# Row sums of a 64 MB tensor: which rows each partition owns

## The chip, the cores and the metric

The kernel runs on one core of one Trainium2 chip. The metric is the device time of one execution in microseconds (us). Before the change the median of three runs is 161.98 us (161.95 to 162.12).

## What is computed

The reference sums each row of 1024 numbers and multiplies the sum by 0.5.

```python
batch, seq, dim = 32, 512, 1024
x = np.random.randn(batch, seq, dim).astype(np.float32)
return (np.sum(x, axis=-1) * multiplier).astype(np.float32)   # multiplier 0.5
```

There are 16384 rows of 4 KB each: 67.1 MB are read, 64 KB are written.

## The kernel before

The 16384 rows are shared out to 128 partitions, 128 rows each. A partition owns 112 consecutive rows of the first 14336 (`x_rows`, `out_rows`: partition p starts at row 112p) and 16 consecutive rows of the last 2048 (`x_last`, `out_last`: partition p starts at row 14336 + 16p). All 128 sums of a partition are gathered in one tile `res`, from which two stores go out.

The loop at line 95 runs over seven blocks of 16 columns. Each round allocates a tile `xb` (128 partitions x 16 rows x 1024 numbers, 8.4 MB) from a pool of three buffers and loads it with one DMA from SyncE's queue (line 98). A partition's part of such a load is 16 rows that lie one after the other in DRAM, 64 KB. VectorE sums the tile with one reduction (line 100) and scales the sums into `res` (line 103). In the seventh block VectorE takes rows 0 to 7 only, and ScalarE takes the other eight, a row at a time, with an activation that accumulates (line 74).

The eighth block is the last 2048 rows. It comes in five DMAs of falling size: rows 0 to 7, 8 to 12 and 13 to 14 (line 117), and row 15 in two parts (line 123) into a tile of its own, `end`. Its rows are summed one at a time, on VectorE (line 84) and on ScalarE (line 74). The first 112 columns of `res` are stored while this block is still coming (line 127, the "early" store); the other 16 are stored at the end (line 145).

The order of the work is that of the code, engine by engine. The first three loads find free buffers and wait for nothing; a hook (`start_loads_at_entry`) puts them at the very start of SyncE's program, ahead of its start barrier. Load 4 and later ones wait on SyncE until VectorE (for the last pieces: VectorE, then ScalarE for the early store) has released a buffer. All loads and stores go through the one queue of SyncE.

## Time and profile before

| | us |
|---|---|
| median of the runs | 161.98 |
| span of the profiled execution | 160.2 |
| VectorE busy | 119.3 (74%) |
| ScalarE busy | 17.3 (11%) |
| one reduction of a full tile (line 100) | 17.22 |
| first full tile landed | 21.89 |
| last DMA of the input landed | 157.55 |

The span runs from SyncE's first DMA issue to the last instruction of the profiled execution. The runs' time holds 1.78 us more than it (161.98 - 160.20), which lies around the span. "To landing" is the time from a DMA's issue to the completion of all of its 16 parts; a load that stands behind others in the queue has their time in it too.

### The profile page before, as it was taken

What the parts mean: (1) busy time and instruction counts of PE and PEld (TensorE: products, weight loads), DVE (VectorE), ACT (ScalarE), POOL (GpSimd) and SP (SyncE); (2) the same over time, 40 slices, a digit from 0 to 9 for tenths busy, and PEclk for the clock granted to TensorE, in tenths of its full rate; (3) what the DMA queues carried; (4) which work ended last, traced back from release to release, by engine and by line L of the source; (5) the groups of instructions that cost most, each with busy time, mean ns of one, the idle gap of its engine ahead of it and who ended that gap; (6) DMA issues with size and microseconds to landing.
All of it is one profiled execution on the core that took longest, in us unless ns stands there. A gap on an engine that the chain in (4) does not pass through costs nothing.

```text
span 160.2 us, 139 instructions
## 1 busy us (share of the span) xinstructions
DVE 119.3 (74%) x35; ACT 17.3 (11%) x31; POOL 0.2 (0%) x4
## 2 busy tenths in 40 slices
DVE  0000059998799968999599995999959999597543
ACT  0000000000000000000000000000000000599952
POOL 0000000000000000000000000000000000000000
DMA  8996996996996997997998989979969969999992
GB/s 278 507 524 262 524 524 262 524 524 262 524 507 278 524 475 311 524 442 344 524 425 360 524 360 425 524 327 458 524 295 491 524 278 507 393 401 422 424 395 76
DMA packets 2016, 67.18 MB, mean 419 GB/s; under 512 B 480, under 2 KB 608, under 8 KB 736
## 3 DMA queue, kind: packets, MB, share of 16 engines
q1 hardware_dynamic: 2016, 67.18, 97.6%
HBM read 67.11 MB, written 0.07 MB: 419 GB/s over the span
## 4 chain that ended last, share of the span: by engine, by line
DMA 75%; DVE 22%; SPq 1%; issue 0%; DVEq 0%
DMA xb<-in_x_dram 51%; DMA end<-in_x_dram 24%; DVE sums L100 22%; SPq L117 1%; SPq L123 0%; DVE end L84 0%; SPq L98 0%; DVE res L103 0%; DVEq L208 0%
## 5 line engine op out<-in xcount | busy, mean ns | idle before, releaser
L100 DVE TENSOR_REDUCE sums<-xb 128x16 f32<-128x16384 f32 (+1 forms) x7 | 112.0, 16002 | 31.5 <-DMA xb<-in_x_dram 31.5
L74 ACT ACT_TABLE_LOAD x1 | 1.3, 1283 | 138.0 <-DMA xb<-in_x_dram 138.0
L74 ACT ACTIVATE xb<-xb 128x1024 f32<-128x1024 f32 x15 | 15.7, 1044 | 2.1 <-DMA xb<-in_x_dram 2.1
L84 DVE CUSTOM_DVE_ANT_0 xb<-xb 128x512 f32<-128x512 f32 x8 | 5.1, 690 | 4.9 <-DMA xb<-in_x_dram 4.9
L74 ACT ACTIVATION_READ_ACCUMULATOR xb<-xb 128x1 f32 x15 | 2.8, 187 | 0.0
L55 DVE MEMSET end<- 128x2 f32 x1 | 0.1, 60 | 1.8 <-PEq L194 1.8
L103 DVE TENSOR_SCALAR res<-sums 128x16 f32<-128x16 f32 (+1 forms) x7 | 1.2, 174 | 0.2
L84 DVE CUSTOM_DVE_ANT_0 end<-end 128x272 f32<-128x272 f32 (+1 forms) x2 | 0.9, 426 | 0.2 <-DMA end<-in_x_dram 0.2
L84 DVE DVE_READ_ACCUMULATOR2_ANT res<- 128x1 f32 x9 | 0.7, 83 | 0.0
L194 POOL MEMSET const-bfloat16-1.0<- 128x1 bf16 x1 | 0.1, 102 | 0.0
L194 POOL MEMSET const-uint8-127<- 128x1 uint8 x1 | 0.1, 102 | 0.0
L194 POOL MEMSET const-float32-0.0<- 128x1 f32 x1 | 0.1, 99 | 0.2 <-issue 0.2
L194 POOL MEMSET const-float32-1.0<- 128x1 f32 x1 | 0.1, 99 | 0.0
L84 DVE DVE_READ_ACCUMULATOR2_ANT end<- 128x1 f32 x1 | 0.1, 83 | 0.0
## 6 DMA issues: line engine op xcount, KB each, us to landing
xb<-in_x_dram SPq DMA_DIRECT2D x1, 4096.0 KB, 31.1
xb<-in_x_dram SPq DMA_DIRECT2D x1, 2560.0 KB, 36.9
xb<-in_x_dram SPq DMA_DIRECT2D x1, 1024.0 KB, 38.9
end<-in_x_dram SPq DMA_DIRECT2D x1, 272.0 KB, 39.0
end<-in_x_dram SPq DMA_DIRECT2D x1, 240.0 KB, 39.2
xb<-in_x_dram SPq DMA_DIRECT2D x7, 40.8
out_dram<-res SPq DMA_DIRECT2D x1, 56.0 KB, 10.0
out_dram<-res SPq DMA_DIRECT2D x1, 8.0 KB, 1.4
```

The source lines that it names most:

```text
L55: nc.vector.memset(end[:, at - 2 : at], 0.0)
L74: acts.append(nc.scalar.activation(out=t[:, r, :], in_=t[:, r, :], func=mybir.ActivationFunctionType.Copy, scale=mul, accum_out=res[:, col ...
L84: return nc.vector.tensor_tensor_reduce(out=row[:, 0:mid], in0=row[:, 0:mid], in1=row[:, mid:], scale=scale, scalar=0.0, op0=ADD, op1=ADD, ...
L100: nc.vector.reduce_sum(out=sums[:, c0 : c0 + h], in_=t[:, 0:h, :], axis=mybir.AxisListType.X)
L103: nc.vector.tensor_single_scalar(out=res[:, c0 : c0 + h], in_=sums[:, c0 : c0 + h], scalar=mul, op=mybir.AluOpType.mult,)
L117: nc.sync.dma_start(out=t[:, lo:hi, :], in_=x_last[:, lo:hi, :])
L194: nc = _bacc.Bacc("TRN2", target_bir_lowering=False, num_devices=1)
```

## The change

```diff
     own = rows - B
-    x_rows = x_flat[0 : P * own, :].rearrange("(p c) d -> p c d", p=P)
+    x_rows = x_flat[0 : P * own, :].rearrange("(b g c) d -> g b c d", b=4, c=own)
     x_last = x_flat[P * own : N, :].rearrange("(p c) d -> p c d", p=P)
-    out_rows = out_flat[0 : P * own].rearrange("(p c) -> p c", p=P)
+    out_rows = out_flat[0 : P * own].rearrange("(b g c) -> g b c", b=4, c=own)
...
-        loads.append(nc.sync.dma_start(out=t, in_=x_rows[:, c0 : c0 + B, :]))
+        loads.append(nc.sync.dma_start(out=t, in_=x_rows[:, :, c0 : c0 + B, :]))
```

The first 14336 rows are still cut into 128 runs of 112 rows. Run number r went to partition r; now run 32b + g goes to partition 4g + b (b from 0 to 3, g from 0 to 31). So four neighbouring partitions own runs that are 32 runs (14.7 MB) apart, and partitions 4 apart own neighbouring runs (458,752 bytes apart). The early store writes the sums back by the same rule. The tiles in SBUF, the sums, the scaling and the last 2048 rows are as they were.

## Prediction

> **What bounds the kernel now.** I read the page first: the busy shares, the slices and the DMA queue.

> ```profile
> span 160.2 us, 139 instructions
> ## 1 busy us (share of the span) xinstructions
> DVE 119.3 (74%) x35; ACT 17.3 (11%) x31; POOL 0.2 (0%) x4
> ...
> DMA  8996996996996997997998989979969969999992
> ...
> q1 hardware_dynamic: 2016, 67.18, 97.6%
> ```

> The busiest engine is at 74%, while the one DMA queue holds its 16 engines for 97.6% of the span. The 9s and 6s of the DMA row are long packets booked in the slice where they start, not gaps. Next the chain that ended last, in order of time:

> ```profile
> 0.00 0.38 SPq L98
> 0.38 0.05 issue
> 0.43 40.77 DMA xb<-in_x_dram
> ...
> 118.38 39.17 DMA end<-in_x_dram
> 157.55 0.02 issue
> 157.58 0.41 DVE end L84
> ```

> It starts with SyncE's first issue, ends with the last transfer landing at 157.55, and is a DMA at both ends. The two reductions in its middle are there only because a load waits for a buffer before it queues up behind others. That this wait costs nothing is read from the timeline, where each reduction starts when its tile has landed, and from VectorE's waits:

> ```profile
> 21.91 17.22 DVE L100 TENSOR_REDUCE sums<-xb 128x16 f32<-128x16384 f32 x1 [20.04 <-DMA xb<-in_x_dram]
> ...
> 41.23 17.22 DVE L100 TENSOR_REDUCE sums<-xb 128x16 f32<-128x16384 f32 x1 [1.89 <-DMA xb<-in_x_dram]
> ...
> 60.58 17.22 DVE L100 TENSOR_REDUCE sums<-xb 128x16 f32<-128x16384 f32 x1 [1.92 <-DMA xb<-in_x_dram]
> ```

> Tiles come every 19.35 us (21.91 to 41.23 to 60.58), VectorE needs 17.22 + 0.17 and idles the other 1.9. A buffer is free at 39.3, and by then the queue still holds the rest of load 2 and all of load 3, some 21 us of work. The kernel is one stream of input with a start and an end.

> The trace's packet records show the stream from inside. Each load is 128 packets of 64 KB, 8 per DMA engine. Load 1 takes 2.52 us a packet in the mean, loads 2 to 7 take 2.42 each, from 2.418 to 2.460. That evenness says that each engine runs at its own pace (65,536 B in 2.418 us, 27.1 GB/s, 434 GB/s for 16) and none waits for memory. The only uneven packets are the first of each engine: 16 packets that start between 1.01 and 1.51 us, take 2.77 to 3.47 (mean 3.21), and end between 3.97 and 4.62. Every later packet follows at its engine's pace, so the start's delay is carried to the end.

> By the profile: 21.89 until load 1 has landed + 6 x 19.345 to load 7 (137.96) + 19.59 for the last block (157.55) + 0.02 + 0.41 for the last sum + 2.2 for the last store and the end = 160.2; the 1.78 around the span make 161.98.

> **The change, part by part.**

> *Bytes, packets, sums.* Nothing is added or removed: seven loads, 64 KB contiguous per partition, the same 7 reductions, 7 scalings, activations and stores. Cost 0.

> *The addresses read at one time.* An engine's packets keep their partitions; what moves is where in DRAM the 16 engines stand at one time. If an engine serves groups of four neighbouring partitions, engines stood 4 x 448 KB = 1.75 MB apart and now stand 448 KB apart. In 48 packets in a row (loads 2 to 7) the old spacing costs nothing that can be seen: 2.418 is the floor in all six loads. The last block, unchanged, has a spacing of 4 x 64 KB, and its 32 KB packets take 1.213 us, also 27.0 GB/s. So two spacings, one wider and one narrower than the new one, run at full pace, and I take 0 for the stream. The lower bound is 0 too (the floor can't fall below what each engine shows alone: 2.414 between starts); the upper bound is far, and is rival A.

> [...]

> *The start.* The first 16 packets take 0.79 us more than later ones in the mean. Some of it belongs to any first read: the six 8 KB instruction fetches that the records show ahead of the span take 0.44 to 0.56 us, where 8 KB in the stream takes 0.31 to 0.32, so 0.12 to 0.25 more. The rest, about 0.6, may be 16 engines meeting at memory. If the new spacing took all that away, the last engine would end its first packet at 1.51 + 2.42 + 0.25 = 4.18 instead of 4.62: a gain of 0.44. If it were twice as bad, a loss of 0.6. I take 0: the same spacing of addresses stands at all later packets and costs nothing there, so the start's excess comes more likely from starting than from the spacing.

> Only the first load pays this: its packets start at 1.01, 0.63 after its issue ends, with no work in the queue before. It moves the whole stream by 0.22. Loads 2 and 3 are issued behind it with 19 us of transfers queued. The entry of SyncE grows from 1.33 by 0.66, which delays the start barrier; VectorE's memset at 1.81 waits on that, but VectorE's first tile lands at 21.89. Loads 4 to 7 are issued into a queue with some 21 us of work. Without that cover, each would cost 0.22.

> *The early store.* 128 packets of 448 B at 25 ns, 8 per engine, 0.2 us of each engine, as before. On SyncE it is issued at 147.79; behind it stand only the wait for the last loads (157.55) and the last store, 9.4 us of cover. Cost 0.

> *Sum.* 160.20 + 0.22 = 160.42 in the profile; 161.98 + 0.22 = 162.20 us in the runs. No stall changes place: VectorE still waits 1.9 per tile.

> **Rivals.**

> *A: the stream gets slower.* If the new addresses make engines meet at memory, or if the two-dimensional source is dealt to the engines differently, so that two write through one way into SBUF, packets take longer than 2.418. Each engine has 56 such packets, all on the path, so 1 ns per packet costs 0.056 us; 6 ns (0.25%) is enough for 0.2% of the time. At 1% more (24 ns) the time is 162.20 + 1.35 = 163.6; if all packets were like the first ones (+0.79), +44 us; if pairs shared one way, 56 x 2.418 = +135 us. It also has VectorE as a limit that stays away: its tile of 17.4 is hidden in all of these. Against it: both neighbouring spacings run at the floor.

> [...]

> *B: the start gets faster.* The first packets meet less. The time is 161.98 + 0.22 - 0.44 = 161.76, or 161.54 if the issue costs nothing as well. It decides when the last first-packet ends before 4.4 us. For it: the excess beyond a lone read, 0.6, is there. Against it: the even stream.

> *C: the change does nothing measurable.* Issue 0, start 0: 161.98. It is the lower end of my forecast case.

> **How the numbers follow.** A measurement of this kernel can tell about 0.2% (0.32 us) from no change. Forecast with C, the stream as it is and an issue that costs 0 to 0.38 or a little more: 0.50; its point of 0.22 lies inside 0.2%, its upper third outside: 0.32 same, 0.18 slower. Rival A: 0.24, of which 0.23 slower, 0.01 same, most of it small. Rival B: 0.26, 0.21 faster (it includes a stream floor that falls a little, which I have no row for), 0.05 same. Together faster 0.21, same 0.38, slower 0.41. The range goes from 161.5 (B at its best) to 163.0 (issue 0.38 and a start 0.6 worse: 162.96; or A with 14 ns per packet). Half of A and a little of B lie outside. The likeliest case alone has 161.98 to 162.36.

> **What would show it.** SyncE's first issue should grow from 0.38 to about 0.6 and the isolated ones from 0.33 likewise; the first reduction should start about 0.2 later than 21.91; the reductions should still be 19.35 apart, and VectorE's idle time before each 1.9. Wrong if packets of loads 2 to 7 leave 2.418 (A), if the first packets end well before 4.6 (B), or if the issue keeps its 0.38 (C).

## The result, and the profile after

The changed kernel takes 162.79 us (median of four runs, 162.64 to 162.84) against 162.00 for the one before: 0.79 us more, a ratio of 1.0049 with a 95% interval of 1.0034 to 1.0063. The prediction was 162.2 with a range of 161.5 to 163.0: the range holds the time and the direction is right, but the change costs over three times the 0.22 that the sum gave, and it is slower by more than 0.2%, for which the text had a chance of 0.41 while its point lay within 0.2%.

The page of after, the lines that answer to those of before:

```profile
span 161.1 us, 139 instructions
## 1 busy us (share of the span) xinstructions
DVE 119.3 (74%) x35; ACT 17.3 (11%) x31; POOL 0.2 (0%) x4
...
q1 hardware_dynamic: 2016, 67.18, 97.1%
```

The engines do what they did (VectorE 119.3 and ScalarE 17.3 in both); the span is 0.9 longer and the queue's share is 97.1% instead of 97.6%. So the time is not in the work. The chain that ended last, in order of time (start, length, what), and VectorE's reductions in the timeline:

```profile
0.00 0.66 SPq L98
0.66 0.05 issue
0.70 41.37 DMA xb<-in_x_dram
...
119.24 39.16 DMA end<-in_x_dram
158.40 0.04 issue
158.44 0.41 DVE end L84
```

```profile
22.75 17.22 DVE L100 TENSOR_REDUCE sums<-xb 128x16 f32<-128x16384 f32 x1 [20.02 <-DMA xb<-in_x_dram]
...
42.10 17.22 DVE L100 TENSOR_REDUCE sums<-xb 128x16 f32<-128x16384 f32 x1 [1.92 <-DMA xb<-in_x_dram]
...
61.45 17.22 DVE L100 TENSOR_REDUCE sums<-xb 128x16 f32<-128x16384 f32 x1 [1.92 <-DMA xb<-in_x_dram]
```

The first reduction starts at 22.75 instead of 21.91, 0.84 late. The next are 19.35 apart with 1.92 of idle time before them, as in before, and the last transfer lands at 158.40 instead of 157.55, 0.85 late. Nothing was lost between: all of it is there when load 1 lands.

The issues of line 98 in the answer for tile xb (min/median/max in ns), before and then after:

```profile
L98 SPq DMA_DIRECT2D xb<-in_x_dram x7: 327/328/432, 0.0 to 97.2; - x7
```

```profile
L98 SPq DMA_DIRECT2D xb<-in_x_dram x7: 534/536/656, 0.0 to 98.0; - x7
```

Isolated issues went from 0.33 to 0.54, the first (the first line of each chain) from 0.38 to 0.66. That is 0.27 for the one that counts, and leaves some 0.6 of the 0.84. The packet records of load 1 have the rest:

| first packet of each of the 16 engines, us | before | after |
|---|---|---|
| starts | 1.01 to 1.51 | 1.44 to 1.72 |
| takes (mean) | 2.77 to 3.47 (3.21) | 2.89 to 3.88 (3.21) |
| ends | 3.97 to 4.62 | 4.36 to 5.49 |
| all 64 KB packets behind them, mean | 2.420 | 2.420 |

The packets start 0.4 us later in the mean (1.56 instead of 1.15). Their mean duration did not change, but the ends are spread over 1.13 us instead of 0.65. Load 1's last packet ends at 21.53 before and at 22.39 after, 0.86 later, and VectorE starts on it 0.84 later, so the end of the slowest first packet (0.87 later) is what counts. From its end to the last landing there are 152.93 us before (157.55 - 4.62) and 152.91 after (158.40 - 5.49).

### The profile page after: what moved, and what is told of

It reads as the page before. It is cut to its first block, busy times and chain, and to the rows that moved or that the text cites. A ratio compares the mean times of both kernels' runs of the same rounds, so it can differ in the third digit from the quotient of the medians.

```text
span 161.1 us, 139 instructions
## 1 busy us (share of the span) xinstructions
DVE 119.3 (74%) x35; ACT 17.3 (11%) x31; POOL 0.2 (0%) x4
## 2 busy tenths in 40 slices
DMA packets 2016, 67.18 MB, mean 417 GB/s; under 512 B 480, under 2 KB 608, under 8 KB 736
## 3 DMA queue, kind: packets, MB, share of 16 engines
q1 hardware_dynamic: 2016, 67.18, 97.1%
## 4 chain that ended last, share of the span: by engine, by line
DMA 75%; DVE 22%; SPq 1%; issue 0%; DVEq 0%
DMA xb<-in_x_dram 51%; DMA end<-in_x_dram 24%; DVE sums L100 21%; SPq L117 1%; SPq L98 0%; SPq L123 0%; DVE end L84 0%; DVE res L103 0%; DVEq L208 0%
## 5 line engine op out<-in xcount | busy, mean ns | idle before, releaser
L100 DVE TENSOR_REDUCE sums<-xb 128x16 f32<-128x16384 f32 (+1 forms) x7 | 112.0, 16001 | 31.5 <-DMA xb<-in_x_dram 31.5
L84 DVE CUSTOM_DVE_ANT_0 xb<-xb 128x512 f32<-128x512 f32 x8 | 5.1, 689 | 5.0 <-DMA xb<-in_x_dram 5.0
L84 DVE CUSTOM_DVE_ANT_0 end<-end 128x272 f32<-128x272 f32 (+1 forms) x2 | 0.9, 426 | 0.2 <-DMA end<-in_x_dram 0.2
L84 DVE DVE_READ_ACCUMULATOR2_ANT res<- 128x1 f32 x9 | 0.7, 83 | 0.0
L84 DVE DVE_READ_ACCUMULATOR2_ANT end<- 128x1 f32 x1 | 0.1, 83 | 0.0
```

The lines of the kernel that those rows point to most:

```text
L84: return nc.vector.tensor_tensor_reduce(out=row[:, 0:mid], in0=row[:, 0:mid], in1=row[:, mid:], scale=scale, scalar=0.0, op0=ADD, op1=ADD, ...
L100: nc.vector.reduce_sum(out=sums[:, c0 : c0 + h], in_=t[:, 0:h, :], axis=mybir.AxisListType.X)
```

## The experiments

Theory I: the longer issue of load 1 is the whole loss. Theory II: the issue makes one half, and the addresses at which the 16 engines start make the other. Rival III (the prediction's rival A): every load pays a little. All times are medians; before, run beside them on the same chip, is 161.98 to 162.02. The distances between engines, here and in the expectations, rest on the prediction's supposition that an engine serves four neighbouring partitions. No trace shows which partitions an engine serves; what the runs vary is the number of rows from partition to partition.

**Where in the stream: load 1 or the others.** Load 1 keeps the old pattern, all others have the new one (`e1_first_old`); then the reverse (`e2_first_new`, with the two sources exchanged, and the two stores' targets with them):

```diff
-        loads.append(nc.sync.dma_start(out=t, in_=x_rows[:, c0 : c0 + B, :]))
+        src = x_rows[:, c0 : c0 + B, :] if b == 0 else x_new[:, :, c0 : c0 + B, :]
+        loads.append(nc.sync.dma_start(out=t, in_=src))
...
-    early = nc.sync.dma_start(out=out_rows, in_=res[:, 0:own])
+    early0 = nc.sync.dma_start(out=out_rows[:, 0:B], in_=res[:, 0:B])
+    early = nc.sync.dma_start(out=out_new[:, :, B:own], in_=res[:, B:own])
```

> Load 1 keeps the old pattern (128 counted steps, the mark, the old addresses), loads 2 to 7 have the new one; the early store is cut in two, so that each part goes to the rows its columns came from. Theory I (all of the loss is the start of load 1, and comes from its issue): 162.0 us, the first issue 0.38 us, the first reduction at 21.9, the issues of loads 2 to 7 0.54 or more and costing nothing. Theory II (the loss is at the start, half from the issue, half from the addresses that the 16 first packets read): 162.0 too. Rival III (the new addresses or the longer issues cost in every load): 162.6 to 162.8, the reductions still later with each load.

> The mirror image: only load 1 has the new pattern, loads 2 to 7 the old one; the early store is cut in two. Theories I and II: the whole loss, 162.8 us, first reduction at 22.7. Rival III: 162.0 to 162.2.

Measured: 162.08 (ratio 1.0008, 0.9999 to 1.0016) and 162.96 (1.0059, 1.0046 to 1.0073). The answer for tile xb shows six long issues (median 536) and a short first one (378) in e1_first_old, and the reverse in e2_first_new:

```profile
L101 SPq DMA_DIRECT2D xb<-in_x_dram x7: 378/536/689, 0.0 to 97.3; - x7
```

```profile
L101 SPq DMA_DIRECT2D xb<-in_x_dram x7: 327/328/666, 0.0 to 98.4; - x7
```

Six loads with the new addresses and the longer issues cost nothing that can be told from noise (162.08), and one, the first, costs all of it (162.96). Rival III falls.

**Issue or addresses.** `e3_first_unmarked` is the kernel before with load 1 built without the mark; `e4_first_near` is the kernel before with load 1 at 28 rows from partition to partition, in a plain pattern with the mark, so that partitions 0, 4, 8 and so on read from where they read in after (that an engine's first packet belongs to one of these is supposed, not shown):

```diff
+        nc.dge_precook = b > 0          # e3
         loads.append(nc.sync.dma_start(out=t, in_=x_rows[:, c0 : c0 + B, :]))
```

```diff
+    x_near = x_flat[0 : P * 28, :].rearrange("(p c) d -> p c d", p=P)      # e4
...
-        loads.append(nc.sync.dma_start(out=t, in_=x_rows[:, c0 : c0 + B, :]))
+        src = x_near[:, 0:B, :] if b == 0 else x_rows[:, c0 : c0 + B, :]
+        loads.append(nc.sync.dma_start(out=t, in_=src))
```

> The kernel before with one thing changed: load 1 is issued without the mark of a shape prepared at build time; addresses and pattern are the old ones. Theory I: nearly the whole loss, 162.6 to 162.8 us, first issue about 0.6 us, first packets ending as late as after the change (5.5 us). Theory II: 162.3 to 162.4, the first packets start 0.2 to 0.4 later but take no longer than before (last end 4.9 to 5.0). Rival III: 162.0 to 162.3.

> The kernel before with one thing changed: load 1 reads partition p from row 28p instead of 112p, with the plain pattern and the mark kept. [...] The first 16 columns are sums of other rows. Theory I: 162.0 us, first packets as before (last end 4.6 us). Theory II: 162.3 to 162.4, first issue 0.38, but first packets take up to 3.9 us and the last ends at about 5.0. Rival III: 162.0.

Measured: e3 162.28 (1.0017, 1.0008 to 1.0026), e4 162.49 (1.0034, 1.0022 to 1.0047). Added, 0.28 + 0.49 = 0.77 of the 0.79. Theory II had expected 162.3 to 162.4 for both: the issue costs a little less than that and the addresses a little more. The beginning of the chain of e3, then of e4:

```profile
0.00 0.54 SPq L99
0.54 0.06 issue
0.59 40.92 DMA xb<-in_x_dram
41.52 0.02 issue
41.54 17.23 DVE sums L101
```

```profile
0.00 0.37 SPq L100
0.37 0.06 issue
0.43 41.18 DMA xb<-in_x_dram
41.61 0.02 issue
41.63 17.23 DVE sums L102
```

In e3 the issue takes 0.54 and load 2's reduction starts at 41.54 instead of 41.23; in e4 the issue is as short as ever (0.37) and the reduction starts later still, at 41.63. In the packet records e3's first packets start late (1.32 to 2.25) and end at 4.33 to 4.88, no more spread than before (0.55); e4's have the old earliest start (1.00) and end at 4.07 to 5.02 (0.95). About a third of the loss (0.28 of 0.77) comes from load 1 without the mark, whose packets start later, and two thirds (0.49) from its addresses, with which the last first packet ends later. Theory I falls; theory II holds, though not with equal halves. Two things stay loose: load 1's issue in after is 0.12 longer than in e3, which the second counted dimension may account for (not tried alone), and e2's time is 0.17 above that of after (first reduction at 23.1, where 22.7 was expected), with overlapping intervals.

**Which addresses.** Only load 1's distance between partitions changes, in the plain pattern of e4: in `P * 28` the 28 becomes 16, 113, 29, 20 or 56; or the whole pattern is moved (`x_flat[4096 : 4096 + P * 28, :]`).

> As the run with 28 rows (plain pattern, mark kept, only load 1 touched, first 16 columns sums of other rows), with 16 rows from partition to partition: load 1 reads one unbroken 8.4 MB, engines 256 KB apart (2^18 bytes). Theory N (the nearer the engines read, the worse the first packets): 162.5 to 162.8 us, last first packet ends at 5.0 us or later. Theory L (it is the lowest address bits in which the engines differ: above bit 18 as before good, bits 16 and 17 bad): 162.0, last end 4.6. Theory P (no order, each set of addresses has its own luck): anything from 161.8 to 162.6.

> The same with 113 rows instead of 112 from partition to partition: engines are as far apart as before (1.77 MB), but their addresses differ from bit 14 up instead of bit 18. Theory N: 162.0 us, last end 4.6. Theory L: 162.5 or more, last end 5.0 or later. Should differing low bits help instead (engines spread over more of memory at once): 161.6 to 161.8, last end 4.2 to 4.4.

> The same with 29 rows: engines as near as after the change (464 KB), addresses that differ from bit 14 up. Theory N: 162.5 us as with 28 rows. Theory L: 162.5 or more. Should differing low bits help: below 162.3, last end under 4.8.

> Only load 1 touched, plain pattern, mark kept, first 16 columns sums of other rows: 20 rows from partition to partition (engines 320 KB apart). 16 rows cost nothing, 28 and 29 cost 0.49 us, 112 and 113 nothing. If the bad distances are a band around 450 KB: 162.0 to 162.2 us. If every distance but multiples of 256 KB and long ones is bad: 162.5.

> The same with 56 rows (engines 896 KB apart, twice the distance after the change). A narrow band around 450 KB: 162.0 us. A loss that fades between 450 KB and 1.75 MB: 162.2 to 162.4.

> 28 rows from partition to partition as in the run of that distance, but the whole pattern starts 4096 rows (16.8 MB) further on. If the distances between the engines make the loss: 162.5 us, last first packet ends at 5.0. If the absolute addresses do: another time, 162.0 as likely as 162.5.

| rows from partition to partition in load 1 | time, us | ratio, 95% interval | last first packet ends, us |
|---|---|---|---|
| 16 | 162.11 | 1.0006, 0.9997 to 1.0015 | 4.58 |
| 20 | 162.19 | 1.0014, 1.0005 to 1.0023 | 5.07 |
| 28 | 162.49 | 1.0034, 1.0022 to 1.0047 | 5.02 |
| 28, moved by 4096 rows | 162.61 | 1.0036, 1.0023 to 1.0048 | 5.36 |
| 29 | 162.50 | 1.0035, 1.0023 to 1.0048 | 5.04 |
| 56 | 162.56 | 1.0036, 1.0022 to 1.0050 | 5.09 |
| 112 (before) | 162.00 | | 4.62 |
| 113 | 162.06 | 1.0003, 0.9994 to 1.0012 | 4.63 |

Nearness (theory N) falls with 16 rows, the lowest differing address bit (L) with 113. A narrow band around 450 KB falls with 56 rows, which cost as much as 28. What is left is a broad band that begins between 16 and 28 rows and ends between 56 and 112, or no order at all (P); the runs do not decide between them. The cost is about the same for 28 and 29 rows and for both places of 28, so neither the exact distance matters there nor this move of the whole pattern. The move is 2^24 bytes, which leaves the low 24 bits of every address as they were; other moves were not tried. Why 28 to 56 rows are bad and 16 and 112 are not is open. No distance tried was better than the one before. The last column is one profiled execution each; that of 20 rows took 162.42, above its median of 162.19.

**Does the start have to be from rest?** Load 1 is cut in two, one 4 KB row per partition from the old addresses first, then 15 rows from the near ones (`e11_row_then_near`) or from the old ones (`e12_row_then_old`):

```diff
+        if b == 0:
+            loads.append(nc.sync.dma_start(out=t[:, 0:1, :], in_=x_rows[:, 0:1, :]))
+            loads.append(nc.sync.dma_start(out=t[:, 1:B, :], in_=x_near[:, 1:B, :]))   # e12: x_rows
```

> Load 1 in two DMAs, both plain and marked: first one row (4 KB) per partition from the old addresses, then the other 15 rows at 28 rows from partition to partition (rows 1 to 15 of a partition are other rows). If the addresses cost only when all engines begin at once from rest, the 4 KB packets take the start and the near addresses cost nothing: the same as the run with the old addresses behind the row, 162.0 to 162.3 us. If the near addresses cost whenever the engines first turn to them: 0.3 to 0.5 more than that run.

> The control: the same two DMAs, the 15 rows from the old addresses. All results are those of the kernel before. Theory I and II: 162.0 us, or up to 0.3 more for 8 more packets per engine and a second issue; if small first packets make the start gentler, down to 161.7.

Measured: 162.12 (1.0009, 1.0000 to 1.0018) and 161.99 (1.0000, 0.9991 to 1.0008). The chain of e11, then of e12, where load 1 has landed and load 2's reduction starts:

```profile
0.90 40.58 DMA xb<-in_x_dram
41.47 0.02 issue
41.50 17.23 DVE sums L105
```

```profile
0.89 40.33 DMA xb<-in_x_dram
41.22 0.02 issue
41.24 17.23 DVE sums L105
```

Behind a row of small packets the near addresses cost 0.13 in the medians instead of 0.49, which is hardly clear of noise. In e11's records 14 of the 16 engines run their first near packet of 60 KB at exactly 2.267 us, the duration that all of e12's have; the other two take 2.31 and 2.34 and are among the first to start. What e11 lost in its profiled execution (41.50 instead of 41.24) is there before the last engine begins its near packets: the row's own packets, at the same old addresses in both runs, end at 3.69 in e11 and at 3.39 in e12, and none of them that starts after the first near packet (2.82) takes longer than 0.159. So in these runs most of the 0.49 belongs to the start from rest, and one row of 4 KB packets is enough to take all but 0.13 of it up. The second issue costs nothing (e12: 161.99 against 161.98), but the start with small packets gains nothing on the old addresses either.

## Why the prediction was right or wrong

*The stream (taken as 0): right.* After and e1_first_old both have the other 64 KB packets at 2.420 in the mean, as before, and none of the 880 takes longer than 2.472; the dearest case of rival A, packets of twice the length, is out. That two engines could share a way into SBUF was the author's supposition; no run shows such a thing. Nor did the new addresses win anything in the stream: e1_first_old, with loads 2 to 7 at them, takes 162.08 against 162.00.

*The issue (0.22): right in kind, its size partly by luck.* No trace shows what the mark does within an issue, so the reason given for 0.22, a shape that has to be worked out, was the author's estimate; the runs show the price. The first issue grew by 0.27 (0.38 to 0.66), and losing the mark alone cost 0.28 in the runs (e3_first_unmarked). But in e3 the issue itself is only 0.15 longer, while its first packets start 0.3 (earliest) to 0.5 us later (mean). So the price is not simply the added length of the issue, as the sum had it. The cover named for the other issues held: loads 2 to 7 pay 0.2 each (median issue 0.54 instead of 0.33 in e1_first_old), and the time is 162.08. VectorE's memset moved from 1.81 to 2.67 and cost nothing, since its first tile is there at 22.75 only.

*The start (taken as 0, bounds -0.44 to +0.6): the step that failed.* It is worth +0.49 in the runs (e4_first_near), near its upper bound. The reason given for 0 was that a spacing which costs nothing in the stream costs nothing at the start. That does not follow: the new spacing costs nothing that can be told from noise in loads 2 to 7 either (162.08), and 0.49 in load 1. e11_row_then_near shows the difference: behind even one row of 4 KB packets the same addresses cost 0.13, and from rest they cost 0.49. Why is open: no run shows the mechanism. That the engines must first get out of step has no support in the records: e11's near packets begin over 0.87 us (2.82 to 3.69), e4's over 1.06 (1.00 to 2.06).

The prediction also split the start's excess into a part of "any first read" (0.12 to 0.25) and a rest. The records do not bear out a fixed part: the latest first packet starts at 2.25 in e3, at 2.17 with 16 rows and at 1.92 with 113, and takes 2.42 to 2.43, hardly more than 2.418. The slow ones are among those that start earlier.

That 0.49 lies within the bounds, and the time within the range, is partly luck. The upper bound was the 0.6 of excess doubled in every first packet; in e4 their mean hardly moved (3.21 to 3.24), and the slowest one grew from 3.47 to 3.77. And the case that came true, a slower start, had a price in the range but no rival and no chance: all the weight of "slower" lay on a longer issue and on rival A. Of that, 0.18 was for an issue of more than 0.32 us; in a range of 0 to 0.38 that is the upper sixth, not the upper third, unless the "little more" is large.

*Rival B had the sign wrong:* the first packets' ends spread more (1.13 instead of 0.65), not less. Rival C is out by the issue alone (0.38 to 0.66). The sign that showed the loss, the last first packet's end against 4.6, had been named for a gain only; the other, a first reduction 0.2 later, came out at 0.84.

## What to carry to other kernels

In this kernel, one uninterrupted DMA stream, what delayed the end of the slowest engine's first packet was paid in full (0.87 there, 0.85 at the last landing), and the longer issues of later loads were covered by the queue (e1_first_old). So look at the first issue and at the first packet of every engine apart from the rest. The source pattern with a second counted dimension, built without the mark, made isolated issues 0.2 us longer (0.33 to 0.54); put such a pattern on loads with a queue ahead of them and keep the first load plain (e1_first_old: 162.08). Evenness in the steady state did not tell how 16 engines get on when they start from rest: later packets take 2.420 in the mean before and after, while the slowest first one went from 3.47 to 3.88.

## What the runs showed of the hardware that was not expected

- Built without the mark, load 1 has an issue that is 0.15 us longer (0.38 in before, 0.54 in e3_first_unmarked), yet its first packets start 0.3 (earliest, 1.01 to 1.32) to 0.5 us later (mean 1.15 to 1.61).
- The 16 engines' first packets from rest took 2.77 to 3.47 us in before and 2.89 to 3.88 in after, where later ones take 2.420 in the mean. The end of the last one changed with the rows from partition to partition: 4.58 to 4.63 us at 16, 112 and 113, 5.02 to 5.36 at 20 to 56 (one profiled execution each).
- In these two runs the spread then stayed: the ends of the 16 engines' packets lie 0.65 us apart after the first and 0.65 after the 56th in before, 1.13 and 1.07 in after. The delay of the last first packet (0.87) is still there at the last landing, 153 us on (0.85).
